# One sum pass per mLSTM head: squares and denominators of both token halves folded to 64 partitions

## The chip, the cores and the metric

The kernel runs on one core of a Trainium2 chip. The metric is the device time of one execution in microseconds (us). Engines are named as in the profile: PE is TensorE's matmul, PEld its weight load, DVE is VectorE, ACT is ScalarE, POOL is GpSimd, SP is SyncE, which issues nearly all DMAs.

## The reference, cut to what matters

The layer has 1024 tokens and a model width of 1024. Four mLSTM heads of width 128 stand beside eight forgetting-attention heads; cross attention, an MLP and a final norm follow. The change touches the end of an mLSTM head, where each token's numerator is divided by a bounded denominator and then normalised over the head's 128 channels:

```python
den = scores.sum(-1) + inter * jnp.einsum('bhd,bhtd->bht', n, qc)
h = num / jnp.maximum(jnp.abs(den), jnp.exp(-m_t))[..., None]
...
mh = mh * lax.rsqrt(jnp.mean(mh * mh, axis=-1, keepdims=True) + EPS)
```

It also touches the RMS norm of the 256 memory tokens, `rmsnorm(mem, ln_mem)`.

## The kernel before, in words

Nearly all matrix products are in float32r, each as three passes over high and low parts (`mm3`, lines 192 to 194). The stages follow one another: projections of the values, then four mLSTM heads, then forgetting attention, the rest of the output projection, cross attention and the MLP.

`ml_project(hd)` makes a head's queries, keys, gate and carried state. `ml_head(hd, ...)` computes the head itself in two token halves of 512 (`hf` 0 and 1). In a half, four key blocks `j` pass through these steps: three score matmuls into a bank `sc`; an exponential on ACT (line 596); a causal mask on POOL (598); the product with the scores on DVE (599); a cut into high and low parts (138, 139); the running sum `acc` of the weights on POOL (603); and three value matmuls into the bank `num`, which is the tile `ov` of the profile.

In `acc` the partitions are keys and the columns are tokens. A token's denominator is therefore the sum of a column over partitions. The same holds for the squares `sq` of the numerator, whose partitions are channels. `sum_cols` (line 232) takes such sums on TensorE: a block of 128 columns is the stationary operand, a column of ones the moving one, and the result has one token per partition. Each half of a head does this for `acc` and for `sq`, four blocks each. ACT then takes the absolute values (618), DVE copies the sums of squares (619), and a chain of small instructions ends in the factor `fac`. In the next call of the generator `to_row` (256 to 261) turns `fac` into rows by way of DRAM, and lines 640 to 645 scale and store the head's output.

Buffers come from rings with few slots. `r_b`, `r_c`, `r_d`, `r_e`, `r_f`, `r_a` and `r_p` have two slots of 128x512 each. `r_b` serves the second half's `acc` (`den1`), the first half's `acc`, the key weights `kw` of the next head's carried state (loaded at line 541), and the value projection of forgetting attention. That last one is `token_major(..., fv_sink)`: sixteen products `t`, whose results leave their PSUM bank through `r_b`, `r_p` and `r_c` in turn (141, 142) before they are stored (664). `r_c` serves the exponentials, `sq` and others. PSUM has the banks `sc` (three), `ov` (one), and for projections `mm`, `m2` (`m` in the profile) and `tp` (two), taken in turn.

The order of each engine's instructions is fixed when the kernel is built: a planner follows the order of the program, runs ahead with what its model of time finds ready, and hands out the slots. Where `in_order()` stands, the order of the program is kept; the mLSTM heads are outside of it. At run time every engine, and SP's queue of DMAs, works its list in order.

`mem_prepare` sums the squares of the memory tokens in two parts of 256 columns side by side and adds the parts on TensorE: `rsqrt_sums(acc, rcol_m, 2, 2)` issues two matmuls for each of two token blocks (line 249).

Of the kernel before, what the change touches and what calls it, by code (L numbers as in the profile page):

```python
# [11 lines left out]
AF = mybir.ActivationFunctionType  # L12
ALU = mybir.AluOpType
# [4 lines left out]
P = 128  # L18
# [4 lines left out]
NM = 256  # L23
# [21 lines left out]
def hybrid_layer(ctx: ExitStack, tc: tile.TileContext, a: dict, out: bass.AP):  # L45
    nc = tc.nc
    v, s, g = nc.vector, nc.scalar, nc.gpsimd
# [11 lines left out]
    def sb(tag, shape, bufs, dt=F32):  # L59
        return pool.tile(shape, dt, tag=tag, name=name(tag), bufs=bufs)  # L60
# [18 lines left out]
    def w2(tag, n=512, dt=F32, p=P):  # L79
        return sb("r_" + tag, [P, 512], BUFS[tag], dt)[:p, :n]  # L80

    def col(tag, n=1, bufs=3):
        return sb("c_" + tag, [P, 8], bufs)[:, :n]
# [3 lines left out]
    def ps_tile(tag):  # L87
        return psum.tile([P, 512], F32, tag=tag, name=name(tag), bufs=PBUFS[tag])

    def sc():  # L90
        return ps_tile("sc")
# [4 lines left out]
    def ov_():  # L96
        return ps_tile("ov")
# [10 lines left out]
    def const(n, shape, dt=F32):  # L108
        return pool.tile(shape, dt, tag=n, name=n, bufs=1)
# [7 lines left out]
    for _ in range(11):  # L117
        nc.tensor.matmul(spun, blank[:, :P], blank, start=True, stop=True)

    ones = const("ones", [P, 1])  # L120
    g.memset(ones, 1.0)
    ident = const("ident", [P, P])
    g.memset(ident, 1.0)
    g.affine_select(out=ident, in_=ident, pattern=[[-1, P]], compare_op=ALU.is_equal, fill=0.0, base=0, channel_multiplier=1)
# [10 lines left out]
    def split(hi, lo, src, scale=None):  # L135

        if scale is None:
            s.activation(hi, src, AF.Copy)  # L138
            return v.tensor_tensor(out=lo, in0=src, in1=hi.bitcast(F32), op=ALU.subtract)  # L139
        else:  # L140
            s.activation(hi, src, AF.Copy, scale=scale)
            return v.scalar_tensor_tensor(out=lo, in0=src, scalar=scale, in1=hi.bitcast(F32), op0=ALU.mult, op1=ALU.subtract)
# [53 lines left out]
    def both(pair, f):  # L196
        return f(pair[0]), f(pair[1])
# [32 lines left out]
    def sum_cols(ps, src, n):  # L230
        for t in range(n):
            nc.tensor.matmul(ps[:, t : t + 1], src[:, t * P : (t + 1) * P], ones, start=True, stop=True)

    def square_sum(acc, x, first, by=s, add=v):
        sq = acc if first else w2("c")[:, : x.shape[-1]]
        if by is s:
            s.activation(sq, x, AF.Square)
        else:
            by.tensor_tensor(out=sq, in0=x, in1=x, op=ALU.mult)
        if not first:  # L240
            add.tensor_tensor(out=acc, in0=sq, in1=acc, op=ALU.add)

    def rsqrt_sums(acc, r, nt, parts=1, bank=None, over=None, how=rsqrt_cols):

        ps = (bank or ov_)()
        for t in range(nt):
            for e in range(parts):
                at = (e * nt + t) * P
                nc.tensor.matmul(ps[:, t : t + 1], acc[:, at : at + P], ones, start=e == 0, stop=e == parts - 1)
        return how(r, ps[:, :nt], 1.0 / D, nt, over)  # L250
# [36 lines left out]
    rcol_m = const("rcol_m", [P, 2])  # L287

    def mem_prepare():
        acc = w2("b")  # L290
        for i in range(KT // 2):
            if i == 2:
                yield
            raw = w2("f")
            load(raw.rearrange("p (k c) -> p k c", k=2), a["mem"][:, 2 * i : 2 * i + 2])
            hi = w2("p", dt=F32R)
            with tc.issue_after(begun):
                square_sum(acc, raw, i == 0)
                for e in range(2):
                    c = slice(e * NM, e * NM + NM)  # L300
                    gain = vec[:, VEC["ln_mem"] + 2 * i + e :][:, 0:1]
                    split(hi[:, c], raw[:, c].bitcast(F32R), raw[:, c], gain)
            for p_, t in enumerate((hi.bitcast(F32), raw)):
                load(hmd[:, p_, 2 * i : 2 * i + 2], t.rearrange("p (k c) -> p k c", k=2))
        yield
        rsqrt_sums(acc, rcol_m, 2, 2)
        to_row(row_m, rcol_m, 2, rowd[1:2, :NM])
        yield

# [7 lines left out]
    def mv_of(hd, t):  # L317

        return mv[hd // 2][:, t, hd % 2 * 256 : hd % 2 * 256 + 256]
# [15 lines left out]
    for k in range(KT):  # L335
        if k % 2 == 0:
            c = slice(k % 4 * 256, k % 4 * 256 + 512)
# [44 lines left out]
    z, e, q, lf = (small[:, i:j].rearrange("p (t c) -> p t c", c=c) for i, j, c in ((0, 128, GC), (128, 224, GW), (224, 320, GW), (320, 416, GW)))  # L382
# [58 lines left out]
    ps = ov_()  # L441
# [135 lines left out]

    def ml_head(hd, q, k, og, num1, den1):
        fac = col("fac", 8)
        nums = []  # L580
        dens = col("dens", 8)
        sqs = col("sqs", 8)
        for hf in range(2):
            nmb = w2("a")
            load(nmb, rows[hd : hd + 1, hf * TH : hf * TH + TH].broadcast_to([P, TH]))
            num = ov_()
            acc = den1 if hf else w2("b")
            last = 4 * hf + 3
            for j in range(4 * hf, last + 1):
                d0 = j - 4 * hf  # L590
                c0 = min(d0 * P, 256)
                sp = sc()
                ks = both(k, lambda z: z[:, j * P : (j + 1) * P])
                mm3(sp[:, c0:], ks, both(q, lambda z: z[:, hf * TH + c0 : hf * TH + TH]), True, True)
                wt = acc if j == 0 else w2("c")
                s.activation(wt[:, c0:], nmb[:, c0:], AF.Exp, bias=gcol[:, j, hd : hd + 1])
                n_ = d0 * P + P - c0
                g.affine_select(out=wt[:, c0 : c0 + n_], in_=wt[:, c0 : c0 + n_], pattern=[[1, n_]], compare_op=ALU.is_ge, fill=0.0, base=c0 - d0 * P, channel_multiplier=-1)
                v.scalar_tensor_tensor(out=wt[:, c0:], in0=sp[:, c0:], scalar=float(P) ** -0.5, in1=wt[:, c0:], op0=ALU.mult, op1=ALU.mult)
                wh, wl = w2("d", dt=F32R), w2("e", dt=F32R)  # L600
                split(wh[:, c0:], wl[:, c0:], wt[:, c0:])
                if j:
                    g.tensor_tensor(out=acc[:, c0:], in0=wt[:, c0:], in1=acc[:, c0:], op=ALU.add)
                vj = mv_of(hd, j)
                mm3(num[:, c0:], (vj[:, :P], vj[:, P:]), (wh[:, c0:], wl[:, c0:]), d0 == 0, j == last)
            sq = w2("c")
            if hf:
                nsb = num1
                v.tensor_tensor(out=nsb, in0=num, in1=nsb, op=ALU.add)
                s.activation(sq, nsb, AF.Square)  # L610
            else:
                nsb = w2("f")
                s.activation(nsb, num, AF.Copy)
                s.activation(sq, num, AF.Square)
            ps = sc()
            sum_cols(ps[:, 0:4], acc, 4)
            sum_cols(ps[:, 4:8], sq, 4)
            s.activation(dens[:, 4 * hf : 4 * hf + 4], ps[:, 0:4], AF.Abs)
            v.tensor_copy(sqs[:, 4 * hf : 4 * hf + 4], ps[:, 4:8])
            nums.append(nsb)  # L620
        v.tensor_tensor(out=dens, in0=dens, in1=emc[:, :, hd], op=ALU.max)
        rd = col("rd", 8)
        v.reciprocal(rd, dens)
        v.tensor_tensor(out=sqs, in0=sqs, in1=rd, op=ALU.mult)
        v.tensor_tensor(out=sqs, in0=sqs, in1=rd, op=ALU.mult)
        rsqrt_cols(fac, sqs, 1.0 / P, 8)
        v.tensor_tensor(out=fac, in0=fac, in1=rd, op=ALU.mult)
        yield
        end = hd == MLH - 1
        fbs = [w2("a"), w2("d")] if end else [None, None]  # L630
        at = facd[hd : hd + 1]
        for hf in range(2):
            fb = fbs[hf] or w2("a")
            if hf == 0:
                to_row(fb, fac, 8, at, sc)
            if hf != end:
                load(fbs[1] or fb, at[:, TH:].broadcast_to([P, TH]))
            yield
            y = nums[hf]
            v.scalar_tensor_tensor(out=y, in0=y, scalar=vec[:, VEC["ml_norm"] + hd : VEC["ml_norm"] + hd + 1], in1=fb, op0=ALU.mult, op1=ALU.mult)  # L640
            v.scalar_tensor_tensor(out=y, in0=og[:, hf * TH : hf * TH + TH], scalar=1.0, in1=y, op0=ALU.add, op1=ALU.mult)
            yh, yl = w2("e" if end and hf else "y", dt=F32R), y.bitcast(F32R)
            split(yh, yl, y, 0.5)
            load(mix[hf, 0, :, hd], yh.bitcast(F32))
            load(mix[hf, 1, :, hd], yl.bitcast(F32))
# [59 lines left out]
    for _ in range(2):  # L705
        t = act().rearrange("p a b -> p (a b)").rearrange("p (i c) -> p i c", i=4)
# [403 lines left out]
    for step in fill:  # L1110
        n, e = divmod(halves[0], 2)
# [479 lines left out]
    for at, (b, m) in enumerate(steps):  # L1591
# [14 lines left out]
        x = x2[m // 2][:, m % 2]  # L1606
# [3 lines left out]
        for i, of, y, op in ((1, 1, x22, ALU.add), (5, 5, x22, ALU.add), (7, 7, x22, ALU.add), (6, 6, x22, ALU.add), (2, 1, x11, ALU.add), (4, 5, x21, ALU.subtract), (3, 7, x12, ALU.subtract)):  # L1610
            if of == i:
                held[of] = bank()
            ps = held[of]
# [9 lines left out]
    for i in range(2):  # L1623
        t = act()
# [132 lines left out]
```

## Time and profile before

| what | value |
|---|---|
| time of a run, median of 3 (lowest, highest) | 1513.87 us (1512.62, 1514.52) |
| profiled execution: first to last instruction | 1510.9 us |
| what lies around the span, against the runs | 1.7 to 3.6 us, 3.0 against the median |
| PE busy | 1498.5 us, 99% |
| DVE, ACT, POOL busy | 1097.5, 717.5, 450.6 us |
| mean granted clock of TensorE | 0.998 |

The profile gives the span of one profiled execution, without a run time of its own; so the span is set beside the times of the three runs. A weight load and the matmul behind it are two records, and a float32 product that is not float32r (a sum over ones) shows two records of each kind.

### The profile page before, as it was taken

To read this page: it belongs to the slowest core of one execution; us is meant where nothing else is said; L and a number is where in the kernel's file an instruction comes from. 1 tells how busy PE (TensorE), PEld (TensorE's weight loads), DVE (VectorE), ACT (ScalarE), POOL (GpSimd) and SP (SyncE) were. 2 spreads that over 40 slices of the span, in tenths; PEclk is the share of its full clock that TensorE was granted. 3 is DMA by queue.
4 is the path that set the end of the run, shared out by engine and by line. 5 is a ranking of instruction groups with operands and counts; after the bars stand their busy time and mean duration, and the time that the engine had idled before them with its cause. 6 is when DMAs were issued, how large, how long until landed. Compare 5 with 4: busy or idle time off the path is not lost.

```text
span 1510.9 us, 21868 instructions
## 1 busy us (share of the span) xinstructions
PE 1498.5 (99%) x7708; PEld 1259.5 (83%) x7708; DVE 1097.5 (73%) x1743; ACT 717.5 (47%) x1347; POOL 450.6 (30%) x529
## 2 busy tenths in 40 slices
PE   9999999999999999999999999999999999999997
PEld 8988888889999888888888888888888888888887
DVE  7676676665799875844457988888887788777765
ACT  7343343334788773534444556565656332222134
POOL 0003030413466551001110033344433644343312
PEclk9999999999999999999999999999999999999999
DMA  5332333436889768533334446867766865555623
GB/s 209 117 114 91 115 100 127 129 130 169 279 253 270 218 199 291 198 123 119 119 119 133 154 136 237 281 244 265 272 243 235 352 258 221 223 223 223 251 84 112
DMA packets 114258, 288.33 MB, mean 191 GB/s; under 512 B 12882, under 2 KB 23436, under 8 KB 108516
## 3 DMA queue, kind: packets, MB, share of 16 engines
q1 hardware_dynamic: 113860, 286.83, 56.0%
q8 instruction: 60, 0.98, 0.3%
q14 instruction: 50, 0.41, 0.1%
q10 hardware_dynamic: 288, 0.11, 0.0%
HBM read 194.36 MB, written 92.53 MB: 190 GB/s over the span
## 4 chain that ended last, share of the span: by engine, by line
PE 98%; issue 0%; DVE 0%; DMA 0%; POOL 0%; ACT 0%; POOLq 0%; ACTq 0%; DVEq 0%
PE tp L194 9%; PE tp L193 9%; PE tp L192 9%; PE sc L192 7%; PE sc L194 7%; PE sc L193 7%; PE m L192 6%; PE m L194 6%; PE m L193 6%; PE mm L192 6%; PE mm L193 6%; PE mm L194 6%; PE ov L813 2%; PE ov L192 2%; PE ov L193 2%; PE ov L194 2%
## 5 line engine op out<-in xcount | busy, mean ns | idle before, releaser
L194 PE MATMUL tp<-act,wh 128*128 128x512 f32 (+1 forms) x456 | 178.5, 392 | 0.0
L192 PE MATMUL tp<-act,wl 128*128 128x512 f32 (+1 forms) x456 | 178.5, 392 | 0.0
L193 PE MATMUL tp<-act,wh 128*128 128x512 f32 (+1 forms) x456 | 178.5, 391 | 0.0
L138 ACT ACTIVATE wh<-wr 128x1024 fp32r<-128x1024 f32 (+3 forms) x96 | 92.7, 966 | 95.9 <-PE tp L194 36.6
L139 DVE TENSOR_TENSOR wl<-wr,wh 128x1024 fp32r<-128x1024 f32 (+3 forms) x96 | 113.9, 1187 | 14.5 <-ACT wh L138 14.4
L193 PE MATMUL mm<-act,wh 128*128 128x512 f32 (+1 forms) x320 | 122.6, 383 | 0.0
L192 PE MATMUL mm<-act,wl 128*128 128x512 f32 (+1 forms) x320 | 122.6, 383 | 0.0
L194 PE MATMUL mm<-act,wh 128*128 128x512 f32 (+1 forms) x320 | 122.3, 382 | 0.0
L192 PE MATMUL m<-act,wl 128*128 128x512 f32 (+1 forms) x312 | 119.5, 383 | 0.0
L193 PE MATMUL m<-act,wh 128*128 128x512 f32 (+1 forms) x312 | 118.9, 381 | 0.0
L194 PE MATMUL m<-act,wh 128*128 128x512 f32 (+1 forms) x312 | 118.8, 381 | 0.0
L192 PE MATMUL sc<-act,wl 128*128 128x512 f32 (+1 forms) x268 | 103.8, 387 | 0.0
L193 PE MATMUL sc<-act,wh 128*128 128x512 f32 (+1 forms) x268 | 103.7, 387 | 0.0
L194 PE MATMUL sc<-act,wh 128*128 128x512 f32 (+1 forms) x268 | 103.6, 387 | 0.0
L194 PEld LDWEIGHTS tp<-act,wh 128*128 128x128 f32 x456 | 85.7, 188 | 19.5
L193 PEld LDWEIGHTS tp<-act,wh 128*128 128x128 f32 x456 | 85.8, 188 | 19.0
L192 PEld LDWEIGHTS tp<-act,wl 128*128 128x128 f32 x456 | 85.7, 188 | 19.0
L1491 POOL TENSOR_TENSOR z<-wr 128x256 f32<-128x256 f32 x56 | 50.4, 921 | 147.6 <-DMA wr<-w_ff2q 140.8
L138 ACT ACTIVATE w<-wr 128x768 fp32r<-128x768 f32 (+2 forms) x31 | 25.5, 825 | 133.7 <-PE tp L194 69.2
L138 ACT ACTIVATE wh<-z 128x1024 fp32r<-128x1024 f32 (+2 forms) x55 | 52.5, 956 | 65.0 <-POOL z L1491 28.8
L139 DVE TENSOR_TENSOR wl<-z,wh 128x1024 fp32r<-128x1024 f32 (+2 forms) x55 | 65.9, 1198 | 10.1 <-ACT wh L138 10.1
L194 PEld LDWEIGHTS mm<-act,wh 128*128 128x128 f32 x320 | 60.2, 188 | 12.5
(673 smaller groups left out, 4207.9 us busy)
## 6 DMA issues: line engine op xcount, KB each, us to landing
act<-right SPq DMA_DIRECT2D x35, 1024.0 KB
right<-r_d SPq DMA_DIRECT2D x70, 256.0 KB
right<-w SPq DMA_DIRECT2D x56, 256.0 KB
wr<-w_ff2q SPq DMA_DIRECT2D x28, 512.0 KB
act<-fqk SPq DMA_DIRECT2D x48, 256.0 KB
wr<-w_in SPq DMA_DIRECT2D x20, 512.0 KB
wr<-w_ff SPq DMA_DIRECT2D x20, 512.0 KB
fqk<-r_p SPq DMA_DIRECT2D x32, 256.0 KB
```

The lines of the kernel that those rows point to most:

```text
L138: s.activation(hi, src, AF.Copy)
L139: return v.tensor_tensor(out=lo, in0=src, in1=hi.bitcast(F32), op=ALU.subtract)
L192: nc.tensor.matmul(ps, w[1], x[0], start=first, stop=False, skip_group_check=more)
L193: nc.tensor.matmul(ps, w[0], x[1], start=False, stop=False, skip_group_check=more)
L194: nc.tensor.matmul(ps, w[0], x[0], start=False, stop=last, skip_group_check=more)
L813: nc.tensor.matmul(self.ov[:, c0:], self.fv[:, self.j], t[:, c0:], start=self.j == 0 and t is self.p[1], stop=self.last and t is self.p[0])
L1491: g.tensor_tensor(out=o, in0=x, in1=y, op=op)
```

## The change

- `ones`, a column, becomes three columns: the column of ones, and two more (`pair_ones`). The first of the pair is one on partitions 0 to 63 and zero on 64 to 127, the second the other way round. Two small memsets are added at the start.
- In `ml_head` the sums leave the loop over the halves. The loop stores the numerators and keeps both `acc` tiles. Behind it, for each half: ACT squares the stored numerator; DVE adds partitions 64 to 127 of `acc` onto its partitions 0 to 63 and writes the result to partitions 64 to 127 of a tile `folded`; DVE does the same with the squares into partitions 0 to 63; four matmuls with `pair_ones` as the moving operand give both sums of a token block in two columns.
- One ACT instruction and one DVE copy then read all eight blocks of the head, where there were two of each.
- In `mem_prepare` DVE adds the two parts (128x256), and two matmuls are left of four.

```diff
-    ones = const("ones", [P, 1])
-    g.memset(ones, 1.0)
+    units_ = const("ones", [P, 3])
+    ones, pair_ones = units_[:, 0:1], units_[:, 1:3]
+    g.memset(units_, 1.0)
+    for e in range(2):
+        g.memset(pair_ones[64 - 64 * e : 128 - 64 * e, e : e + 1], 0.0)
...
-        rsqrt_sums(acc, rcol_m, 2, 2)
+        v.tensor_tensor(out=acc[:, :NM], in0=acc[:, :NM], in1=acc[:, NM:], op=ALU.add)
+        rsqrt_sums(acc, rcol_m, 2)
...
-            sq = w2("c")
             if hf:
                 nsb = num1
                 v.tensor_tensor(out=nsb, in0=num, in1=nsb, op=ALU.add)
-                s.activation(sq, nsb, AF.Square)
             else:
                 nsb = w2("f")
                 s.activation(nsb, num, AF.Copy)
-                s.activation(sq, num, AF.Square)
-            ps = sc()
-            sum_cols(ps[:, 0:4], acc, 4)
-            sum_cols(ps[:, 4:8], sq, 4)
-            s.activation(dens[:, 4 * hf : 4 * hf + 4], ps[:, 0:4], AF.Abs)
-            v.tensor_copy(sqs[:, 4 * hf : 4 * hf + 4], ps[:, 4:8])
             nums.append(nsb)
+            accs_.append(acc)
+        ps = sc()[:, :16].rearrange("p (t e) -> p t e", e=2)
+        for hf in range(2):
+            folded = w2("c")
+            sq = w2("c")
+            s.activation(sq, nums[hf], AF.Square)
+            for t, x in ((folded[64:128], accs_[hf]), (folded[0:64], sq)):
+                v.tensor_tensor(out=t, in0=x[0:64], in1=x[64:128], op=ALU.add)
+            for t in range(4):
+                nc.tensor.matmul(ps[:, 4 * hf + t], folded[:, t * P : (t + 1) * P], pair_ones, start=True, stop=True)
+        s.activation(dens, ps[:, :, 1], AF.Abs)
+        v.tensor_copy(sqs, ps[:, :, 0])
```

More of the change, by code (lines that the diff above doesn't have):

```diff
@@ L579, in ml_head @@
         fac = col("fac", 8)
-        nums = []
+        nums, accs_ = [], []
         dens = col("dens", 8)
```

## The prediction

> **What bounds the kernel now.** I read the page first, then what PE waited for, then the stretches of the mLSTM stage.
>
> ```profile
> span 1510.9 us, 21868 instructions
> PE 1498.5 (99%) x7708; PEld 1259.5 (83%) x7708; DVE 1097.5 (73%) x1743; ACT 717.5 (47%) x1347; POOL 450.6 (30%) x529
> PE 98%; issue 0%; DVE 0%; DMA 0%; POOL 0%; ACT 0%; POOLq 0%; ACTq 0%; DVEq 0%
> ```
>
> The chain that ended last lies on PE for 98% of the span. All waits of PE in the whole execution are these (engine, line, what was waited for, us in total, times, longest):
>
> ```profile
> PE ov L228 <- DVE c_r L220: 1.7, 1, 1.7
> PE mm L192 <- DVE act L142: 1.4, 1, 1.4
> PE ov L118 <- DVE r_y L115: 1.2, 1, 1.2
> PE sc L754 <- ACT act L767: 0.7, 1, 0.7
> PE ov L232 <- DVE c_var L1649: 0.5, 1, 0.5
> PE sc L754 <- ACT w L767: 0.4, 1, 0.4
> ```
>
> They add up to 5.9 us, and none is in an mLSTM head. The stage of the heads, and the end of its last head, as stretches (us, then busy time of PE, PEld, DVE, ACT, POOL, granted clock, DMA share, GB/s):
>
> ```profile
> 100.00:400.00 300.00, 298.89 (x1656) 257.12 (x1655) 194.29 (x335) 119.28 (x226) 73.68 (x96) 1.00 0.43 133
> 330.00:362.00 32.00, 32.00 (x262) 31.52 (x261) 16.56 (x34) 14.27 (x32) 12.03 (x15) 1.00 0.52 139
> ```
>
> PE is busy for 298.89 of 300 us at full clock; DVE has 106 us to spare, ACT 181. So a record taken from PE shortens the kernel by its slot, as long as PE finds the next one ready. That condition is where the change can lose.
>
> **The PE records that go.** The sums over ones in the four heads, by the tile that they read, and those of the memory norm:
>
> ```profile
> L232 PE MATMUL sc<-ones,r_b x64: 164/250/250, 127.8 to 356.9; 128*128 128x1 f32 x64
> L232 PE MATMUL sc<-ones,r_c x64: 164/250/250, 140.0 to 360.4; 128*128 128x1 f32 x64
> L249 PE MATMUL ov<-ones,r_b x8: 165/250/250, 95.7 to 96.4; 128*128 128x1 f32 x8
> ```
>
> Four heads with two halves, two sums and four blocks make 64 products and 128 records, so a product is two records. After the change a head has 2 x 4 = 8 products: 32 products, 64 records. The memory norm goes from 8 records to 4. In all 64 + 4 = 68 records go.
>
> What a record costs is not its listed 250 ns, since records overlap, but its share of PE's sequence:
>
> ```profile
> 359.57 0.28 PE L194 MATMUL tp<-wh,act 128*128 128x256 f32 x1
> 359.69 0.95 PE L232 MATMUL sc<-ones,r_c 128*128 128x1 f32 x8
> 360.50 0.36 PE L192 MATMUL m<-wh,act 128*128 128x256 f32 x1
> 360.70 0.28 PE L193 MATMUL m<-wl,act 128*128 128x256 f32 x1
> ```
>
> A matmul of 256 columns starts 0.12 us behind the one before. Eight sums take 359.69 to 360.50, and the matmul behind them takes 0.20 instead of 0.12: 0.81 + 0.08 = 0.89 us, 0.111 each. The bounds are 0.101 (0.81 / 8) and 0.12 (the 256-column slot, which a record of one or two columns doesn't exceed). So **68 x 0.111 = 7.5 us go**, between 6.9 and 8.2. The same bound prices the second column of the moving operand at nothing: even 256 columns need no more than 0.12. The rows of the stationary tile stay 128 (`folded` is full), so that form stays too.
>
> **What is added, off PE.** Sixteen folds on DVE (64x512), one addition of 128x256, two memsets. The nearest rows are the addition of two halves of a tile at line 823, and the instructions that go or shrink:
>
> ```profile
> L823 DVE TENSOR_TENSOR r_f<-r_c x16: 686/745/1229, 402.8 to 573.4; 64x512 f32<-64x512 f32 x16
> L619 DVE COPY c_sqs<-sc x8: 147/151/162, 142.8 to 361.7; 128x4 f32<-128x4 f32 x8
> L618 ACT ACTIVATE c_dens<-sc x8: 165/174/174, 140.9 to 361.1; 128x4 f32<-128x4 f32 x8
> L614 ACT ACTIVATE r_c<-ov x4: 591/592/592, 135.1 to 341.9; 128x512 f32<-128x512 f32 x4
> L610 ACT ACTIVATE r_c<-r_f x4: 631/632/632, 156.2 to 356.8; 128x512 f32<-128x512 f32 x4
> ```
>
> DVE: 16 x 0.745 = 11.9 us (11.0 to 19.7 by the row's ends), less 4 copies (0.6): 11.3 us more in a stage where it idles for 106. ACT: four squares read a stored tile instead of the bank (4 x 0.04 more) and four 0.174 us instructions go: about 0.5 us less. The memory addition is a fold-like instruction of half the width, below 0.75 us, once; the memsets are two short instructions at POOL's start, while PE's first product waits for the input anyway (the second of PE's waits). I take all of them at nothing for the end of the kernel: PE doesn't wait for these engines there. If that cover is gone, a head's end is later by its four folds, 3.0 us.
>
> Two things are released earlier: the bank `ov` after the first half's copy alone (the square at 614 went to the same bank, 0.59 us), and the `sc` bank that held the first half's sums.
>
> **What is held longer.** The first half's `acc` sits in one of two `r_b` slots, now until its fold at the head's end and no longer until its sums in the middle. Two users wait for that slot.
>
> First, in heads 0 to 2, the load of the next head's `kw`. It waits on SP's queue already:
>
> ```profile
> SPq L541 <- PE sc L232: 13.6, 3, 5.6
> 132.85 0.32 SPq L541 DMA_DIRECT2D r_b<-left  x1
> 141.16 0.33 SPq L180 DMA_DIRECT2D wr<-w_in  x1
> 159.27 0.28 PE L551 MATMUL tp<-act,r_e 128*128 128x256 f32 x1
> ```
>
> It is loaded at 132.85, and the state products made from it are on PE at 159.27. The head's second square stands at 156.2 now (first start in the row of line 610), so the fold comes near 155, the load 22 us later than now, and these products, by my estimate, 5 to 10 us later. Only the carry needs them; PE has the next head's projections to put in their place. Behind a blocked SP queue stand the weights (141.16), and these are loaded two projections ahead. I take this at nothing; its upper bound is the third rival's.
>
> Second, in head 3, the first value projections for forgetting attention:
>
> ```profile
> 340.67 0.47 ACT L141 ACTIVATE r_b<-tp,rcol 128x256 fp32r<-128x256 f32 x1 [1.17 <-PE sc L232]
> 347.48 2.11 POOL L603 TENSOR_TENSOR r_b<-r_c,r_b 128x384 f32<-128x384 f32 x2 [0.28 <-DVE r_c L599]
> 350.85 0.29 DVE L761 TENSOR_REDUCE c_mx<-sc 128x1 f32<-128x128 f32 x1 [0.94 <-PE sc L734]
> 357.37 0.46 ACT L141 ACTIVATE r_c<-tp,rcol 128x256 fp32r<-128x256 f32 x1
> ```
>
> The product that fills bank `tp` first is read out at 340.67, after ACT waited 1.17 us for the sums of `acc`, which set `r_b` free. Now `r_b` comes free with the fold of `acc`. That fold needs no square, only a slot of `r_c`; POOL's third addition of weights ends at 349.59 and frees one, and DVE then stands idle for 0.94 us. So the fold ends near 351.5, 11 us after the present read-out. Until then one `tp` bank is held, the other waits for `r_c` until 357.37 in any case, and a fifth product has no `tp` bank. PE's work of that kind between 330 and 361 us, by bank:
>
> ```profile
> L192 PE MATMUL tp<-wh,act 128*128 128x256 f32 x32 | 9.0, 282 | 0.0
> L192 PE MATMUL mm<-wh,act 128*128 128x256 f32 x16 | 4.5, 279 | 0.0
> L192 PE MATMUL m<-wh,act 128*128 128x256 f32 x10 | 2.9, 288 | 0.0
> ```
>
> With lines 193 and 194 that is 172 records. The first four products (96 records) have banks of their own; the other 76 x 0.12 = 9.1 us are cover that PE may lack between about 347.5 and 361. A slot that comes at 351.5 takes 4 of these 13.5 us, in proportion 2.7 us. The sixth product goes to bank `mm`, which is free, and fits: 24 x 0.12 = 2.9 us. PE's list does mix products on two banks:
>
> ```profile
> 364.82 0.28 PE L192 MATMUL mm<-wh,act 128*128 128x256 f32 x1
> 365.53 0.28 PE L192 MATMUL tp<-wh,act 128*128 128x256 f32 x1
> ```
>
> So the loss lies between 0 (all replaced) and 9.1 us (slot only at the head's end). I take **0.7 us**, a quarter of the 2.7, since mixing is what the planner already does.
>
> **The sum.** -7.5 + 0.7 = -6.8 us on the profiled execution, 1510.9 to 1504.1. The runs' median is 3.0 us above that span, which I keep: 1513.9 - 6.8 = **1507.1 us**, 0.45% faster. From the bounds, the likeliest case by itself runs from 1505.7 (-8.2) to 1509 (6.9 gained, 2 lost).
>
> **Rivals.**
>
> *PE starves at the end of head 3 (slower).* Place: PE between 347.5 and 361, banks `tp` held by products whose results wait for `r_b`. If the planner puts the fold of `acc` with the rest of the head's end, the whole 9.1 us shows: 1513.9 - 7.5 + 9.1 = 1515.5; with the end itself later by its folds (3.0), 1518.5. It decides from a slot that comes free after about 359 us (7.5 of the 9.1). For it: line 141 waits for exactly this release now. Against: the fold has what it needs by 350, and the planner counts slots. In part (2.5 to 6 us lost) it gives 1509 to 1512.4.
>
> *The folds are late on DVE.* These rows show what a fold does to its neighbours:
>
> ```profile
> 402.04 0.68 DVE L139 TENSOR_TENSOR r_e<-tp,r_d 128x512 fp32r<-128x512 f32 x1
> 402.75 1.23 DVE L823 TENSOR_TENSOR r_f<-r_c 64x512 f32<-64x512 f32 x1
> 403.90 0.41 DVE L761 TENSOR_REDUCE c_mx<-sc 128x1 f32<-128x256 f32 x1
> ```
>
> The instruction behind line 823 starts 0.08 us before that one's end; line 823 itself starts 0.03 us after the end of the one before, 0.11 us worse. Four folds at the longest, 4 x (1.23 + 0.11) = 5.4 us, end a head 2.4 us later than my 3.0. Uncovered in head 3, that is 1507.1 + 2.4 = 1509.5. Covered, as the 16.56 busy of 32 us suggest, it is nothing.
>
> [...]
>
> *SP's queue is blocked by `kw`.* If its load keeps its place at 132.85, SP stands until the fold, near 155 to 160. The stores of projections behind it come late, their `r_p` slots and then PSUM banks are held. At 5 us in each of three heads: 1507.1 + 15 = 1522. Against: these waits are 13.6 us in three now and PE shows none.
>
> *No gain, since two columns or the folded form cost more.* The 256-column slot of 0.12 us excludes it but for a rest: 1513.9.
>
> *Another order elsewhere.* The planner's other choices may shift; the largest waits of the kind at the start of the attention stage are 0.7 and 0.4 us. A few of them give 1509 to 1510.
>
> **How the numbers follow.** The likeliest case 0.60; PE starved in full 0.09, in part 0.13; late folds 0.07; SP blocked 0.03; no gain 0.01; another order 0.07. A change of 0.2% (3.0 us) is about what a measurement of this kernel tells from none, so faster means below 1510.9: 0.60 + 0.07 + 0.07 and half of the partial starvation, 0.80; I lower it to 0.76 for what a trace of before can't show of the planner. Same: the rest of the partial one, no gain, and the full one below 1516.9: 0.13, with the lowering 0.14. Slower: the full one above that, the blocked queue and the lowering: 0.10. The range is 1505.5 to 1513.5: it leaves out the full starvation, the blocked queue and a little below.
>
> **What would show it.** Right: 64 records on PE over `folded`, 4 in the memory norm, PE's busy time lower by about 7 us, no PE wait between 330 and 365 us above 1 us, the first `r_b` read-out near 345 to 352. Wrong: a PE wait for ACT or DVE there, or folds far above 0.75 us with PE behind them. A span lower by less than 3 us with 68 records gone would mean that PE lost its cover; the list of PE's waits names the place.

## The result, and the profile after

The changed kernel takes 1509.78 us (median of 15 runs, 1507.26 to 1511.67) against 1513.4 us for the kernel before on the same chip (1512.01 to 1514.52): a ratio of 0.9976, interval 0.9969 to 0.9982. Two later comparisons gave 0.9968 [0.9957, 0.9980] and 0.9975 [0.9965, 0.9986]. So 3 to 5 us are gained, a good half of the 6.8 us forecast. The profiled execution took 1509.8 us, with a span of 1508.0.

The head of the page, the busy times, and the chain of work that ended last:

```profile
span 1508.0 us, 21748 instructions
PE 1494.7 (99%) x7640; PEld 1253.6 (83%) x7640; DVE 1105.4 (73%) x1756; ACT 717.5 (48%) x1343; POOL 451.0 (30%) x531
PE 90%; DVE 3%; DMA 2%; ACT 1%; issue 1%; POOL 1%; SPq 0%; POOLq 0%; DVEq 0%; ACTq 0%
```

7708 - 7640 = 68 records are gone, as counted. PE's busy time fell by 3.8 us, not 7, and a tenth of the chain now lies off PE, where it was 2%. What PE waited for (engine, line, what, us in total, times, longest):

```profile
PE ov L231 <- DVE c_r L223: 1.7, 1, 1.7
PE ov L118 <- DVE r_y L115: 1.2, 1, 1.2
PE sc L626 <- DVE r_c L624: 0.9, 1, 0.9
PE ov L260 <- DVE w L448: 0.8, 1, 0.8
PE sc L762 <- ACT act L775: 0.7, 1, 0.7
PE ov L235 <- DVE c_var L1657: 0.5, 1, 0.5
```

Two of these are new: 0.9 us ahead of the folded sums (line 626 now), and 0.8 us at the transpose of `to_row` (260). The first is in head 3. These are PE's records there, in order of time (start, us, instruction, idle time before it), then the folds on DVE and the read-out of `r_b` on ACT:

```profile
345.70 0.28 PE L197 MATMUL mm<-wh,act 128*128 128x256 f32 x1
346.86 1.05 PE L626 MATMUL sc<-ones,r_c 128*128 128x2 f32 x8 [0.88 <-DVE r_c L624]
347.77 0.37 PE L762 MATMUL sc<-act 128*128 128x256 f32 x1
...
349.14 0.41 PE L197 MATMUL tp<-wh,act 128*128 128x256 f32 x1
349.35 0.41 PE L195 MATMUL tp<-wh,act 128*128 128x256 f32 x1
...
352.00 0.28 PE L196 MATMUL tp<-wl,act 128*128 128x256 f32 x1
352.12 0.28 PE L197 MATMUL tp<-wh,act 128*128 128x256 f32 x1
...
352.94 0.95 PE L626 MATMUL sc<-ones,r_c 128*128 128x2 f32 x8
```

```profile
345.32 0.69 DVE L624 TENSOR_TENSOR r_c<-r_b 64x512 f32<-64x512 f32 x1 [2.02 <-POOL r_b L607]
346.12 0.69 DVE L624 TENSOR_TENSOR r_c<-r_c 64x512 f32<-64x512 f32 x1
346.05 0.47 ACT L144 ACTIVATE r_b<-tp,rcol 128x256 fp32r<-128x256 f32 x1 [2.45 <-DVE r_c L624]
```

The products on the banks `m` and `mm` run out at 345.70. The next of their kind needs a `tp` bank, whose content waits for `r_b` until the fold of `acc` at 345.32 to 346.01. PE's list therefore has the sums of the first half next, and these wait for two folds. Behind them something else is wrong: at 349 the products of 256 columns stand 0.21 us apart, at 352 again 0.12. The same place in two adjoining stretches (us, busy times of PE, PEld, DVE, ACT, POOL, granted clock, DMA share, GB/s):

```profile
345.02:348.43 3.41, 2.53 (x22) 2.26 (x20) 2.85 (x5) 1.10 (x2) 0.27 (x1) 1.00 0.45 88
348.43:351.85 3.42, 3.42 (x18) 3.38 (x17) 2.21 (x6) 1.75 (x6) 0.00 (x0) 0.50 0.45 122
```

For 3.4 us TensorE was granted half its clock. At 0.213 us a record instead of 0.118 that loses 3.41 x (1 - 0.118 / 0.213) = 1.5 us, a loss that no list of waits shows, since PE counts as busy all through. It is 1.5 of the 3.7 us by which the fall of PE's busy time stayed below 7.5.

To place the rest I took, for each record of PE, the time to the start of the next one, less its usual slot (0.118 us for 256 columns, 0.112 for a sum), and summed that by stretches of 25 us. The changed kernel's execution has 4.9 us more of such lost time than that of before: 2.7 at 325 to 375 us (the wait and the half clock), 0.7 in the first 50 us, 0.7 at 425 to 450, 0.5 near 958 and 0.4 near 1186. Those at 425 and 958 come and go between the three traces of the change; the one near 1186 is in all three (0.3 to 0.4 us), and what it is stays open. With the records' 7.5 us: -7.5 + 4.9 = -2.6, against -2.9 between the spans.

### The profile page after: what moved, and what is told of

It reads as the page before. It is cut to its first block, busy times and chain, and to the rows that moved or that the text cites. A ratio compares the mean times of both kernels' runs of the same rounds, so it can differ in the third digit from the quotient of the medians.

```text
span 1508.0 us, 21748 instructions
## 1 busy us (share of the span) xinstructions
PE 1494.7 (99%) x7640; PEld 1253.6 (83%) x7640; DVE 1105.4 (73%) x1756; ACT 717.5 (48%) x1343; POOL 451.0 (30%) x531
## 4 chain that ended last, share of the span: by engine, by line
PE 90%; DVE 3%; DMA 2%; ACT 1%; issue 1%; POOL 1%; SPq 0%; POOLq 0%; DVEq 0%; ACTq 0%
PE tp L195 8%; PE tp L196 8%; PE tp L197 8%; PE m L195 6%; PE m L197 6%; PE m L196 6%; PE sc L196 6%; PE sc L195 6%; PE sc L197 6%; PE mm L195 6%; PE mm L197 6%; PE mm L196 6%; PE ov L821 2%; PE ov L195 2%; PE tp L801 2%; PE ov L197 2%
## 5 line engine op out<-in xcount | busy, mean ns | idle before, releaser
L1499 POOL TENSOR_TENSOR z<-wr 128x256 f32<-128x256 f32 x56 | 54.7, 998 | 141.3 <-DMA wr<-w_ff2q 131.6
```

The source lines that it names most:

```text
L1499: g.tensor_tensor(out=o, in0=x, in1=y, op=op)
```

## The experiments

The theories as they stood. *A*: the 68 records are worth the 7.5 us forecast, and the end of the last head takes half of it back, since the first half's `acc` holds `r_b`. *B*: the records are worth half as much, for instance because two columns cost more than one. *C*: the memory part costs the missing 3.5 us. All ratios are to the kernel before on the same chip, with their intervals.

**The change in pieces.** `heads_only` undoes the memory part:

```diff
-        v.tensor_tensor(out=acc[:, :NM], in0=acc[:, :NM], in1=acc[:, NM:], op=ALU.add)
-        rsqrt_sums(acc, rcol_m, 2)
+        rsqrt_sums(acc, rcol_m, 2, 2)
```

> The memory norm is as before (4 products, no addition on DVE); the heads are as changed. Theory A (the 68 records were worth 7.5 us; the rest was lost in PE waits and in a half clock behind one of them): the memory part loses more than it gains, since its addition stands on DVE ahead of the gates' addition and PE waits 0.9 us near 49 us for that; so this kernel is 0.5 us faster than the changed one, near 1509.3, and that PE wait is gone. Theory B (a sum record costs PE only half of 0.111 us, and the waits are of no account): 4 records return, 0.2 us slower than the changed one, near 1510.

Measured: 1506.25 us, 0.9959 [0.9946, 0.9973], further from the change than A allowed. Its trace still has the wait ahead of the folded sums, but no half clock behind it (the granted clock is 1.00 up to 350.69 us):

```profile
PE sc L625 <- DVE r_c L623: 0.8, 1, 0.8
```

`mem_only` does the memory part alone, in the kernel before (the same lines the other way round).

> The kernel before with the memory part alone: 4 records less (0.45 us), and the addition on DVE ahead of the gates' addition. Theory A: PE waits 0.2 to 0.9 us near 49 us: between 0.2 us faster and 0.5 us slower than before, 1512.5 to 1513.4. Theory C: 2.5 to 3.5 us slower than before, 1515 to 1516.5.

Measured: 1513.91 us, 1.0004 [0.9995, 1.0012]. The part by itself neither costs nor gains anything that can be measured, so C falls as a cost of the part alone. What undoing it gives in the changed kernel must come from how it meets the rest.

`half_end` keeps the fold but not the move: each half squares, folds and sums at its own end.

```diff
-            accs_.append(acc)
-        ps = sc()[:, :16].rearrange("p (t e) -> p t e", e=2)
-        for hf in range(2):
...
+            ps = sc()[:, :8].rearrange("p (t e) -> p t e", e=2)
...
+            s.activation(dens[:, 4 * hf : 4 * hf + 4], ps[:, :, 1], AF.Abs)
+            v.tensor_copy(sqs[:, 4 * hf : 4 * hf + 4], ps[:, :, 0])
```

> Folded, but not moved: each half squares, folds and sums at its own end, 8 products a head as in the change. acc's slot of r_b comes free in the middle of the head again. Theory A: the PE wait of 0.9 us at the last head's sums and the half clock behind it are gone, 2 to 3 us faster than the changed kernel: 1506.5 to 1508. Theory B: as the changed kernel, 1509 to 1510.5.

Measured: 1515.84 us, 1.0024 [1.0014, 1.0033]: slower than before, with the same 7640 records on PE as the change, where A expected 2 to 3 us less than the change. PE's new waits, and the two stretches at the end of head 2:

```profile
PE tp L555 <- DVE r_e L142: 2.8, 2, 1.4
PE sc L624 <- DVE r_c L621: 2.1, 1, 2.1
PE ov L196 <- DVE r_e L142: 1.3, 2, 1.0
```

```profile
295.15:298.57 3.42, 1.17 (x7) 0.96 (x8) 2.77 (x6) 1.23 (x2) 0.53 (x1) 1.00 0.00 0
298.57:301.98 3.41, 3.41 (x13) 3.00 (x12) 1.63 (x4) 0.59 (x2) 0.00 (x0) 0.50 0.00 0
```

Here too a stretch with little for PE to do is followed by 3.4 us of half clock. Folding where the sums stood puts two more tiles into the ring `r_c` and two folds on DVE into the middle of a head, where PE waits for DVE's cuts into high and low parts (line 142 here); all of the gain and 3.6 us more are lost. That the ring and not DVE's time is to blame was not tried apart.

`move_only` moves the sums to the head's end without folding (sixteen products a head, memory part as in the change).

```diff
-            for t, x in ((folded[64:128], accs_[hf]), (folded[0:64], sq)):
-                v.tensor_tensor(out=t, in0=x[0:64], in1=x[64:128], op=ALU.add)
-            for t in range(4):
-                nc.tensor.matmul(ps[:, 4 * hf + t], folded[:, t * P : (t + 1) * P], pair_ones, start=True, stop=True)
+            sum_cols(ps[:, 4 * hf : 4 * hf + 4], accs_[hf], 4)
+            sum_cols(ps[:, 8 + 4 * hf : 12 + 4 * hf], sq, 4)
```

> Moved, but not folded: 16 products a head at the head's end, acc and squares each summed over 128 partitions, memory part as changed. Theory A: 64 records (7.1 us) return beside the losses of the move: 1513.5 to 1517, no faster than before. Theory B: half of that returns: 1512.5 to 1513.5.

Measured: 1514.28 us, 1.0012 [1.0003, 1.0021]. The move without the fold costs 1.8 us. Its trace has no wait above 0.4 us in a head, but it shows one of the faster executions (1513.17 us, at a mean granted clock of 0.997). Of the eleven runs, four have a mean granted clock of 0.995 or 0.996 and take 1515.1 to 1517.5 us, so in these a part of the cost is time at half clock, by the estimate further down. Between the ratio of `move_only` and those of the change (0.9968 to 0.9976) lie 5.4 to 6.7 us, more than B's half price for 64 records, 3.6 us; between the two profiled executions lie only 3.4 us. This pair leans to A and doesn't decide.

**The held slot.** `fv_z` is the changed kernel with every third result of `fv_sink` in another ring, so that no product waits for `r_b`:

```diff
-        o = rotate("b", "p", "c").bitcast(F32R)...
+        o = (rotate("p", "c") if (8 * c + t) % 3 else z4()[:, :512]).bitcast(F32R)...
```

> The changed kernel, with each third result of the value projection of forgetting attention going to a slot of the ring z (idle at that time) instead of r_b. Theory A: the products no longer wait for acc's slot, PE has work until the folded sums of the last head are ready; that wait is below 0.3 us, the clock stays full near 345 to 355 us, and the time falls by 1.5 to 2.5 us to 1507.3 to 1508.3. Theory B: no change beyond 0.5 us, 1509.3 to 1510.3.

Measured: 1506.25 us, 0.9957 [0.9945, 0.9970], 6.5 us faster than before and 1 us better than A allowed. Its trace has no wait at the folded sums and no half clock (between 348.8 and 351.7 us, as between 352.7 and 366, products of 256 columns stand 0.12 us apart). PE's records at the same place:

```profile
346.90 0.28 PE L196 MATMUL mm<-wl,act 128*128 128x256 f32 x1
347.02 0.95 PE L626 MATMUL sc<-ones,r_c 128*128 128x2 f32 x8
347.83 0.36 PE L762 MATMUL sc<-act 128*128 128x256 f32 x1
```

The fifth product has its `tp` bank in time and goes ahead of the sums. Eight sums of two columns take 347.02 to 347.83, the same 0.81 us as those of one column before. Both speak for A: two columns cost no more than one, so B's reason falls, and without the stall most of the forecast gain is there. The free slot is not all that differs, though: with it the planner orders PE's list anew between 342 and 382 us. And `heads_only` keeps the slot held and gains nearly as much (0.0041 x 1512.7 = 6.2 us). What the two traces have in common is a wait of at most 0.8 us at the sums and no half clock.

In the same company, `after_again` is the changed kernel once more, `both` joins `fv_z` and `heads_only`, and `fill` puts eight transposes of 128 columns ahead of the last head's sums, to occupy PE while it waits:

```diff
+        bank_ = sc()
+        if hd == MLH - 1:
+            for t in range(8):
+                nc.tensor.transpose(bank_[:, (2 + t % 2) * P : (3 + t % 2) * P], accs_[1][:, (2 + t % 2) * P : (3 + t % 2) * P], ident)
```

> The changed kernel itself, beside the others on one chip. Theory A (PE idles 0.9 us ahead of the last head's folded sums, and in some executions a 3.4 us stretch at half clock follows, 1.7 us): 1508 to 1511 with a spread of some 3 us. Theory C (the memory part alone costs the 3.5 us by which the kernel without it was faster): the same time, but with a small spread, and without a half clock in the slower runs.

> The memory norm as before, and each third result of the value projection in ring z: both sources of PE waits taken away. Theory A: 0.3 to 1 us faster than either alone, 1505 to 1506, PE busy without a wait over 0.5 us in the heads. Theory C: as without the memory part alone, since nothing else was lost.

> The changed kernel, with eight transposes of 128 columns (0.9 us of PE) in front of the last head's folded sums, whose results are overwritten. They run where PE stood idle. Theory A: the wait is replaced by work of the same length, so that gains nothing, but no half clock follows: 1507.5 to 1508.5, 1 to 2 us faster than the changed kernel although PE does more. Theory C: 0 to 0.9 us slower than the changed kernel.

Measured: `after_again` 1508.35 us, 0.9968 [0.9957, 0.9980], with a wait of 1.6 us and the same 3.4 us at half clock. `both` 1506.4 us, 0.9953 [0.9940, 0.9965]. A expected it 0.3 to 1 us ahead of either alone, and that can't be told from none here: next to `fv_z` the memory part makes no difference that can be measured. `fill` 0.9973 [0.9961, 0.9985]: the 1 to 2 us that it should have won didn't come. The wait at the sums and the half clock behind it are gone from its trace (the granted clock is 1.00 from 348.33 to 351.75 us), but the transposes changed the planner's order, and another product of `fv_sink` stands still where its bank `m` waits for `r_b`:

```profile
PE m L195 <- DVE r_b L145: 1.5, 1, 1.5
```

So the stall was moved, not removed, and `fill` doesn't show that filling a gap keeps the clock.

**Why the memory part matters at all.** Giving the memory sums their four records back makes the planner place some twenty products and a few instructions of DVE and ACT between 97 and 156 us (up to the end of head 0) differently; the lists of head 3 are the same. `mem_pad` tells this from DVE's addition: it keeps the addition, and issues each of the two sums twice into the same place, so that its lists are those of `heads_only` but for the addition.

```diff
-        rsqrt_sums(acc, rcol_m, 2)
+        ps_ = ov_()
+        for t in range(2):
+            for _ in range(2):
+                nc.tensor.matmul(ps_[:, t : t + 1], acc[:, t * P : (t + 1) * P], ones, start=True, stop=True)
+        rsqrt_cols(rcol_m, ps_[:, :2], 1.0 / D, 2, None)
```

> The changed kernel whose two sums of the memory norm are each issued twice into the same place: DVE's addition of 128x256 stays as in the change, and PE has the 8 records of the kernel before. Every engine's list is then that of the version with the memory part undone, but for DVE's addition: with four more records the planner also moves about twenty value projections and a few DVE and ACT instructions in the first two heads back to where that version has them. Theory 'order': the 2 to 3 us that undoing the memory part gained come from those lists and from where the end of the last head then falls, so this kernel is as fast as that version, ratio 0.9955 to 0.9963 to the kernel before, with a PE wait of 0.9 us at most ahead of the last head's folded sums. Theory 'addition': they come from DVE's addition, which delays the gates' addition near 49 us and PE's to_row transpose behind it; then this kernel stays at the change's ratio, 0.9968 to 0.9980, or 0.3 us above.

> The changed kernel once more, beside the other two: ratio 0.9965 to 0.998. If the half-clock stretch at the end of the last head belongs to this kernel's lists, its trace shows it a third time, 3.4 us long, behind a wait of 0.9 to 1.6 us; if it was the chance of two executions, it is as likely missing.

> The version with the memory part undone once more: ratio 0.995 to 0.9965, PE wait near 0.8 us ahead of the last head's folded sums. If its missing half clock belongs to the shorter wait, it is missing again; if it was chance, the trace may show it, and then the ratio's gain over the change must lie elsewhere.

Measured on one chip: `mem_pad` 1507.7 us, 0.9969 [0.9957, 0.9981]; `after_third` 1509.14 us, 0.9975 [0.9965, 0.9986]; `heads_again` 1507.13 us, 0.9964 [0.9951, 0.9976]. The times don't settle it: by its ratio `mem_pad` lies inside what "addition" expected (0.9968 to 0.9980) and outside "order" (0.9955 to 0.9963), but `heads_again` beside it came out at 0.9964, and all three intervals overlap. For the stall in head 3 the traces do take a side. Below are the stretches that hold the first sums of head 3: of `after_again` and `after_third` with the one behind each, then of `heads_only`, `heads_again` and `mem_pad`:

```profile
344.39:347.80 3.41, 1.83 (x16) 1.60 (x14) 2.48 (x5) 1.04 (x2) 0.64 (x1) 1.00 0.39 76
347.80:351.22 3.42, 3.42 (x18) 3.29 (x17) 2.58 (x6) 1.82 (x7) 0.00 (x0) 0.50 0.34 94
```

```profile
345.18:348.59 3.41, 2.01 (x18) 1.90 (x18) 3.05 (x6) 1.22 (x3) 0.00 (x0) 1.00 0.22 46
348.59:352.00 3.41, 3.41 (x19) 3.41 (x18) 1.90 (x5) 1.64 (x6) 0.00 (x0) 0.50 0.53 149
```

```profile
343.86:347.28 3.42, 2.67 (x24) 2.42 (x22) 2.61 (x5) 1.11 (x2) 0.52 (x1) 1.00 0.55 109
347.28:350.69 3.41, 3.41 (x32) 3.37 (x31) 2.45 (x6) 1.75 (x6) 0.00 (x0) 1.00 0.37 104
```

```profile
345.90:349.32 3.42, 2.88 (x25) 2.79 (x25) 3.16 (x7) 1.58 (x4) 0.00 (x0) 1.00 0.43 106
```

```profile
345.90:349.32 3.42, 2.82 (x24) 2.73 (x25) 3.16 (x7) 1.58 (x4) 0.00 (x0) 1.00 0.42 102
```

In all three traces of the change PE waits for 0.9 to 1.6 us at the sums, is busy for 2.53 us or less of that stretch, and the clock is halved behind it. In the three traces with eight memory records it waits for 0.8, 0.5 and 0.7 us, is busy for 2.67 us or more, and the clock stays. `mem_pad` has DVE's addition and yet no half clock: so the half clock in head 3 goes with the lists and not with the addition. What the addition costs elsewhere stays open, and so does why those lists shorten the wait by some 0.5 us.

A trace is one execution, and the length of a wait doesn't tell by itself whether the clock falls behind it: in `after_again` a wait of 1.6 us is followed by 3.4 us at half clock, while in `fill` the 1.5 us at bank `m` end at 352.58 us, and the products behind it stand 0.12 us apart from 352.77 to 357.60. Whether the shorter wait or luck kept the clock in the traces of `heads_only`, `heads_again` and `mem_pad` is not shown by these three executions alone.

The runs speak against luck. By my estimate from two traces, a stretch at half clock of 3.413 us lowers the mean granted clock of a run by 0.5 x 3.413 / 1508 = 0.0011, and the half clock at the end of the kernel, 5.8 us in the trace of the change and 7.3 us in that of the kernel before, lowers it by 0.0019 and 0.0024. So a run listed at 0.998 lost no such stretch, one at 0.996 or less lost at least one, and 0.997, which an end of little more than 7.3 us would give as well, can be either. Of the 29 runs of the change 10 are at 0.998 and 7 at 0.996 or less; of the 26 runs of `heads_only`, `heads_again`, `mem_pad`, `fv_z` and `both` none is below 0.997. In the first comparison the change's four runs at 0.998 take 1507.8 to 1508.8 us, and its four at 0.996 take 1509.4 to 1511.7.

## Why the prediction was right, and where its size was off

- **The records: right.** 64 over `folded` and 4 in the memory norm are left, 68 gone, and the second column costs nothing (0.81 us for eight, before and after). Where the end of the last head loses nothing, the gain agrees with the forecast: `both` lacks 64 records, 64 x 0.111 = 7.1 us, and is 0.0047 x 1513 = 7.1 us faster, with its interval 5.3 to 9.1. The rows of the sums and of the folds in the changed kernel:

```profile
L626 PE MATMUL sc<-ones,r_c x64: 165/251/272, 152.0 to 353.6; 128*128 128x2 f32 x64
L624 DVE TENSOR_TENSOR r_c<-r_b x8: 689/689/691, 146.4 to 347.9; 64x512 f32<-64x512 f32 x8
```

- **The folds on DVE: right.** 0.69 us each (0.745 taken), 16 of them, covered but for head 3, where PE waits for them as part of the 0.9 us. The second of a pair starts 0.03 to 0.11 us behind the first one's end in all eight pairs (345.32 + 0.69 to 346.12 in the rows above). The forecast's price for this, 0.11 us, was the step from 0.08 us before the end to 0.03 behind it; where the second fold starts 0.11 us behind the end, the step is 0.19, which changes nothing in the sum.
- **`kw` and SP's queue: nothing, for a better reason than given.** The load stands at 147.15 us in head 0, 14 us later than before and not 22, and the state products didn't come 5 to 10 us later: they start at 158.6 (159.27 before). In SP's waits and in the first and last start of these products:

```profile
SPq L545 <- DVE r_c L624: 17.5, 3, 6.1
147.15 0.32 SPq L545 DMA_DIRECT2D r_b<-left  x1
L555 PE MATMUL tp<-act,r_e x8: 279/282/367, 158.6 to 294.9; 128*128 128x256 f32 x8
```

- **The end of head 3: the step that was mis-sized.** The mechanism was as told: the slot of `r_b` comes free with the fold (the read-out at 346.05, in the forecast 345 to 352), the product on `mm` is taken ahead, and then work runs out. But the term stood at 0.7 us, and the lost time between 325 and 375 us is 2.7, 4.1 and 3.2 us more than before in the three traces of the change. 0.9 to 1.6 us of it is the wait. 1.5 us is the half clock behind it, which the prediction didn't think of at all: a gap was priced at its length. The rival "PE starves, in part" names this very mechanism, with 2.5 to 6 us, and 1509 to 1512.4 us; the result lies in its lower half, and 0.8 us above the likeliest case's 1509. So what came was the rival with a chance of 0.13, and that the time lies in the range is owed in part to the range having room for it. The prediction's own signs say the same: a PE wait for DVE at the sums, and a span lower by less than 3 us (2.9) with 68 records gone, were its signs of lost cover, and PE's busy time fell by 3.8 us where about 7 was the sign of being right. "No PE wait above 1 us" held for the first trace (0.9) and not for the other two (1.6, 1.4).
- **The memory part at nothing: right by itself, wrong in company.** DVE's addition goes ahead of the gates' addition and delays it, and PE's transpose waits for that (0.8 us in the first trace, 0.2 and none in the others):

```profile
49.56 0.43 DVE L309 TENSOR_TENSOR r_b<-r_b 128x256 f32<-128x256 f32 x1
49.90 0.28 DVE L448 TENSOR_TENSOR w<-w,ov 128x128 f32<-128x128 f32 x1
50.23 0.27 PE L260 MATMUL ov<-ident,rcol 128*8 128x128 f32 x1 [0.77 <-DVE w L448]
```

"PE doesn't wait for these engines there" was thus not quite so. The memsets, at 0.8 to 1.5 us, cost nothing that shows; the wait that covers them is the third of the list, in front of PE's first product at 1.24 us, and not the second, which ends at 7.15. The planner's order above is the other effect of this part.
- **The sum.** -7.5 + 0.7 was forecast; -7.5 + 2.7 to 4.1, and up to 0.7 at the start, is what the traces show. That gives 3 to 5 us, as measured. The 3.0 us that the forecast put on top of the span is a difference between executions: in every run that lists both, the time is 1.7 to 1.9 us above the span, and the profiled execution of the kernel before was the fastest of its three (1512.62).

## What to carry to other kernels

On an engine that is busy for 99%, a record saved is worth its slot (here 64 records of 0.111 us gave 7.1 us, between 5.3 and 9.1), but only where the next record is ready: before moving work to the end of a stage, look for the buffer that it holds until then and for the last independent work in front of it. Price a gap on TensorE not only by its length: here 3.4 us at half clock followed a wait of 0.9 to 1.6 us, and cost 1.5 us more in the first trace. When a change pays half, give back the suspected slot (here another ring for one result in three) before doubting the price of the instructions, and look at the granted clock of every run, since one trace can hold or miss such a stretch.

## What the runs showed of the hardware

In the trace of the change the record of the granted clock starts at full clock at 7.096 us of the span, falls to half at 348.429, is full again from 351.842, and is at half from 1502.134 to the end. In the trace of the kernel before it starts at 5.157 us and falls once, at 1503.608. The half clock in head 3 lasted 3.413 us, and the three falls stand 341.333, 1495.038 and 1498.451 us behind the start of their record: 100, 438 and 439 times that length. Of `after_again` (347.80 to 351.22 us), `after_third` (348.59 to 352.00) and `half_end` (298.57 to 301.98) the traces show stretches of 3.41 to 3.42 us at 0.50 all through.

None of the four stretches just ahead of these was idle: PE was busy for 2.53, 1.83, 2.01 and 1.17 us of 3.41 or 3.42, and the one in the change had 0.9 us of waiting and 0.9 us of two-column sums in it. That busy time doesn't settle it: the first 3.41 us of the clock's record in the kernel before have PE busy for 1.96 us, less than the 2.53 us of the change, and the clock stays full behind them, with products of 272 columns 0.13 us apart up to 11.9 us.

```profile
5.16:8.57 3.41, 1.96 (x14) 1.46 (x13) 2.59 (x8) 2.88 (x10) 0.00 (x0) 1.00 1.02 381
```

What decides whether the clock falls was not shown: no run was made to vary it by itself.
